# Where the split parts of the u/gate weights are kept, when their raw columns are loaded, and a Silu in two parts

## The chip, the cores and the metric

The kernel runs on one core of a Trainium2 chip. The metric is device time in microseconds (us) of one execution. In the text PE is the matrix engine (TensorE), DVE is VectorE, ACT is ScalarE, POOL is GpSimd, and SP is the engine whose queue issues the DMAs.

## The reference, cut to what matters

One inference step of a two-layer trunk over 1088 tokens (1024 of a prompt, 8 x 8 of new tokens), width 1024, fp32. Layer 0 is a gated linear attention and is the same before and after the change. Layer 1 is the one that matters here:

```
h = rmsnorm(x, norm_g[1])
u, v, gate = split(h @ w_in, 3)           # three times 1024 columns
v = layernorm(v, ln_g, ln_b)
mixed = ws (lower triangle, per group) @ v, within chunks of 128 positions, + bias
z = u * mixed * silu(gate)
x = x + z @ w_out
y = rmsnorm(x, norm_final)
```

## The kernel before

**Precision.** Each fp32 operand is split in two parts, `hi` (a copy that the matrix engine reads as fp32r) and `lo` (the rest). A split of a weight block of 128 x 1024 numbers is two halves of work: one ACT copy (`A.activation(w[:, 0], ...)`) and one DVE subtraction (`V.tensor_tensor(w[:, 1], ...)`). A product is three passes: hi.hi, hi.lo and lo.hi.

**The u/gate stage.** A loop over m = 0..7 makes u and gate for 128 columns each, and z for them. It doesn't do eight block products but seven, after Winograd's scheme: the weights of one m are cut in four quarters `q[1,1]`, `q[1,2]`, `q[2,1]`, `q[2,2]` (even and odd k-tiles by u and gate), POOL makes four sums of them (`sums`: s1 = q21+q22, s2 = s1-q11, s3 = q11-q21, s4 = q12-s2, 128 x 512 each), and the activations' sums `tsum` have been made before the loop. The seven products of one m run on the PE in this order, 24 matmuls of 272 columns each:

| product | weights | accumulator | what frees or reads the accumulator |
|---|---|---|---|
| 1 | s2 | `pb` | ACT copies it to `p6` (L1133, tile name `half`) |
| 2 | s3 | `pe` (tile `two`) | ACT copies it to `sg` (L1145) |
| 3 | s1 | `pb`, added to product 1 | DVE adds it to `sg` (L1149) |
| 4 | q11 | `pa` (tile `p1`) | ACT copies it to `p1` (L1156), POOL adds that to `p6` and `sg` (L1158, L1159) |
| mix | v by the spatial weights | two tiles `mix` in the tag "o" (two buffers), then a small third one for the sample tokens | DVE writes `zt` from each (L1102, L1096) |
| 5 | s4 | `pb` | DVE adds it to `p1` (L1174) |
| 6 | q22 | `pe` | DVE makes `sg` of the first half of the tokens from it (L1194) |
| 7 | q12 | `pa` | DVE multiplies it into `zt` (L1215) |

`sg` is the gate. It is multiplied by the tokens' 1/rms (`rs_all`), goes through Silu on ACT (L1198, all 1088 tokens at once), is multiplied by `rs_all` once more, and `zt` is multiplied by it (L1217) and spilled to DRAM (`z_spill`).

Seven tiles hold the split parts of one m (tag "w", eight buffers, `parts_of`, L964 and L965). They are taken **in turn**: each new split goes into the buffer that was used eight splits ago. The raw columns of the next m are loaded by `Quarters(...)` (L959, four DMAs of 256 KB) late in the iteration, after the Silu, into one tile `rawq`; POOL makes s1 and s2 of the next m after product 3, s3 and s4 later, and ACT and DVE split the parts of the next m between product 5 and the first products of the next m.

**What sets the order.** From the v stage to the end of the loop the order is that of the code: `in_order()` ties each instruction to the one before it on its own engine, so on every engine (the SP queue too) nothing passes an instruction that waits. After the loop a scheduler orders the instructions by priority.

**After the loop.** `out_proj(28, ...)` computes x + z @ w_out. Its blocks (p, m) are 24 matmuls for 128 output columns m and a piece p of the tokens (384, 384 or 320 of them), 24 blocks in all; `fm_block` takes an accumulator of the tag "mm" (two buffers, the tag that `pa` uses too). Blocks (0, 0) and (0, 1) come first. They need the four weight tiles of block 28, w28_0 to w28_3 (two k-tiles each, L122 and L123), and `zs[0]`, the splits of z for the first 384 tokens: k-tiles 0 to 4 come from `stage`, 5 and 6 from `rest` (both read back from the spill), 7 from the last `zt`. Even k-tiles can be split once product 3 of m = 7 is done, odd ones after product 5, since both overwrite `act_all`, which these products read. In the last iteration the order on DVE is therefore a mix of the gate's work, seven of these splits, and the splits of w28_0 to w28_2.

Of the kernel before, what the change touches and what calls it, by code (L numbers as in the profile page):

```python
# [40 lines left out]
def trunk_kernel(ctx: ExitStack, tc: tile.TileContext, a: dict):  # L41
# [67 lines left out]

    def load_w(blk, i):  # L110
        n = 256 + (LOW if blk == 1 else 0)
        raws[blk, i] = wp.tile([P, 2, 256 + LOW], F32, tag="raw", bufs=3, name=f"wr{blk}_{i}")[:, :, :n]
# [683 lines left out]
    def out_proj(base, act, resid, done, seq, gain=None):  # L796
# [29 lines left out]
        for item in seq:  # L826
# [141 lines left out]
    class Quarters:  # L968
# [19 lines left out]
        def parts(self, key):  # L988
            self.w[key] = parts_of(self.raw[key])

        def plain(self, *keys):
            for k in keys:
                self.w[k] = parts_of(self.q[k])
# [126 lines left out]
    for m in range(KT):  # L1120
# [9 lines left out]
        p6, p1 = ([tmp(t, 2, QUART, "half") for r in R] for t in ("sq", "hn"))  # L1130
        for r in R:
            product(pb[r], w["s2"], tq[1][r])
            A.activation(p6[r], pb[r], AF.Copy)  # L1133
# [45 lines left out]
        v_out(m, vm, bc)  # L1179
        if more:  # L1180
            nxt.sums("s4", up)
            vm = v_load(m + 1)
# [8 lines left out]
        for r in R:
            product(pe[r], w[2, 2], tq[3][r], start=False)
        for r in R:
            V.tensor_tensor(sg[:, qa[r]], p6[r], pe[r], ALU.add)  # L1194
        if more:
            nxt.plain((1, 1))
        V.tensor_tensor(sg[:, fa], sg[:, fa], rs_all[:, fa], ALU.mult)
        A.activation(sg, sg, AF.Silu)  # L1198
        if more:
            nxt.plain((2, 2))  # L1200
        else:
            fetch_w(28, [1, 2])
        V.tensor_tensor(sg[:, fa], sg[:, fa], rs_all[:, fa], ALU.mult)
        V.tensor_tensor(sg[:, fb], sg[:, fb], rs_all[:, fb], ALU.mult)
        if more:
            nxt.plain((1, 2))
            if m + 2 < KT:
                following = Quarters(22 + m)
            else:
                stage = mp.tile([P, 5, N], F32, tag="rawq", name="zstage")  # L1210
                SP.dma_start(stage, z_d[:, 0:5, 0:N])
                following = None
        for r in R:
            product(pa[r], w[1, 2], b21[r], start=False)
            V.tensor_tensor(zt[:, qa[r]], pa[r], zt[:, qa[r]], ALU.mult)  # L1215
# [157 lines left out]
```

## Time and profile before

| | us |
|---|---|
| median of 3 runs | 950.47 (947.46 to 951.05) |
| the profiled execution | 951.55, of which the span from first to last instruction is 949.8 |
| PE busy | 909.2 of the span |
| DVE, ACT, POOL busy | 630.6, 458.8, 279.8 |
| u/gate loop, first to last product | 636.7 to 829.7 |
| first matmul of `out_proj(28)` | 836.9 |
| start of the last matmuls of the kernel | 938.7 |

The profiled execution is 1.08 us longer than the median. Times in the text are those of its trace, counted from the start of the span. Rows of the timeline give start, duration, engine, line, operation, output and inputs, a count, and in brackets the idle time ahead of it with what ended it. For matmuls the duration of a row reaches to the end of the last one's pipeline, so distances between products are read from their starts.

### The profile page before, as it was taken

What the parts mean: (1) busy time and instruction counts of PE and PEld (TensorE: products, weight loads), DVE (VectorE), ACT (ScalarE), POOL (GpSimd) and SP (SyncE); (2) the same over time, 40 slices, a digit from 0 to 9 for tenths busy, and PEclk for the clock granted to TensorE, in tenths of its full rate; (3) what the DMA queues carried; (4) which work ended last, traced back from release to release, by engine and by line L of the source; (5) the groups of instructions that cost most, each with busy time, mean ns of one, the idle gap of its engine ahead of it and who ended that gap; (6) DMA issues with size and microseconds to landing.
All of it is one profiled execution on the core that took longest, in us unless ns stands there. A gap on an engine that the chain in (4) does not pass through costs nothing.

```text
span 949.8 us, 17088 instructions
## 1 busy us (share of the span) xinstructions
PE 909.2 (96%) x6437; PEld 882.1 (93%) x6437; DVE 630.6 (66%) x1288; ACT 458.8 (48%) x972; POOL 279.8 (29%) x307
## 2 busy tenths in 40 slices
PE   9989999999999999989999999999999999979995
PEld 8979989998999899978999999999999999879994
DVE  7888777577885877688544755465666666772246
ACT  7664644454462545464243545554444444463322
POOL 2023332323222342222242200025554554301123
PEclk9999999999999999999999999999999999979998
DMA  9302113310231212324583344552233233573233
GB/s 297 92 1 81 51 34 89 106 45 29 67 104 59 62 50 78 118 70 127 169 259 112 101 143 144 185 159 82 90 94 95 97 96 97 160 245 101 58 112 129
DMA packets 89968, 101.80 MB, mean 107 GB/s; under 512 B 9863, under 2 KB 80845, under 8 KB 89885
## 3 DMA queue, kind: packets, MB, share of 16 engines
q1 hardware_dynamic: 89884, 100.71, 34.1%
q8 instruction: 50, 0.82, 0.4%
q14 instruction: 34, 0.27, 0.1%
HBM read 74.26 MB, written 26.42 MB: 106 GB/s over the span
## 4 chain that ended last, share of the span: by engine, by line
PE 46%; DVE 24%; DMA 11%; issue 6%; ACT 6%; POOL 5%; SPq 2%; DVEq 0%; POOLq 0%; ACTq 0%
PE fm L137 26%; PE tm L151 10%; DVE wq L965 4%; DMA rawq<-w 3%; DMA xsum<-x_spill 3%; DMA wr<-w 1%; PE sc L513 1%; POOL qsum L977 1%; PE o L623 1%; PE pst L584 1%; SPq L959 1%; POOL half L1158 1%; DVE sg L1183 1%; DMA xt<-x_spill 1%; DVE scT L526 1%
## 5 line engine op out<-in xcount | busy, mean ns | idle before, releaser
L137 PE MATMUL fm<-act,w 128*128 128x384 f32 (+1 forms) x2208 | 390.7, 333 | 7.9 <-DVE zt L1215 7.0
L137 PEld LDWEIGHTS fm<-act,w 128*128 128x128 f32 x2208 | 368.1, 189 | 11.7 <-ACT act L197 7.2
L151 PE MATMUL tm<-w,act 128*128 128x256 f32 (+1 forms) x1536 | 193.1, 283 | 0.9 <-ACT vt L1010 0.6
L151 PEld LDWEIGHTS tm<-w,act 128*128 128x128 f32 x1536 | 185.5, 188 | 2.9 <-ACT vt L1010 1.1
L123 DVE TENSOR_TENSOR w<-wr,w 128x512 fp32r<-128x512 f32 (+1 forms) x96 | 68.1, 724 | 25.1 <-ACT w L122 24.5
L122 ACT ACTIVATE w<-wr 128x512 fp32r<-128x512 f32 (+1 forms) x96 | 58.5, 625 | 31.8 <-DMA wr<-w 19.7
L821 POOL TENSOR_TENSOR acc<-acc,sq 128x384 f32<-128x384 f32 (+1 forms) x30 | 30.4, 1014 | 117.6 <-ACT sq L816 117.2
L843 DVE TENSOR_TENSOR x<-fm,res 128x384 f32<-128x384 f32 (+1 forms) x40 | 21.0, 527 | 56.6 <-PE fm L137 56.6
L999 PE MATMUL pb<-act,wq 128*128 128x272 f32 x384 | 52.1, 292 | 5.3 <-ACT half L1133 5.2
L999 PEld LDWEIGHTS pb<-act,wq 128*128 128x128 f32 x384 | 48.9, 189 | 6.9 <-ACT half L1133 6.9
L816 ACT ACTIVATE sq<-x 128x384 f32<-128x384 f32 (+1 forms) x42 | 20.9, 503 | 63.8 <-DVE x L843 61.6
L999 PE MATMUL two<-tsum,wq 128*128 128x272 f32 x384 | 51.6, 290 | 0.0
L999 PE MATMUL p<-act,wq 128*128 128x272 f32 x384 | 51.0, 288 | 0.0
L999 PEld LDWEIGHTS p<-act,wq 128*128 128x128 f32 x384 | 49.4, 188 | 0.0
L999 PEld LDWEIGHTS two<-tsum,wq 128*128 128x128 f32 x384 | 49.1, 188 | 0.0
L977 POOL TENSOR_TENSOR qsum<-rawq 128x512 f32<-128x512 f32 x16 | 20.6, 1288 | 84.1 <-DMA rawq<-w 81.2
L468 POOL TENSOR_TENSOR xe<-xe,k 128x384 f32<-128x384 f32 (+2 forms) x24 | 29.1, 1212 | 44.3 <-ACT xe L467 41.1
L654 POOL TENSOR_TENSOR on<-on,g 128x384 f32<-128x384 f32 (+1 forms) x24 | 23.8, 1012 | 56.6 <-DVE on L653 34.6
L964 ACT ACTIVATE wq<-qsum 128x512 fp32r<-128x512 f32 x25 | 15.0, 626 | 52.3 <-POOL qsum L977 52.3
L444 POOL TENSOR_TENSOR kd<-kd,k 128x384 f32<-128x384 f32 (+1 forms) x12 | 12.0, 1002 | 85.8 <-ACT kd L443 85.8
L475 DVE TENSOR_TENSOR xl<-cum 128x192 f32<-128x192 f32 (+4 forms) x72 | 34.6, 507 | 0.0
L1102 DVE SCALAR_TENSOR_TENSOR zt<-mix,lng,bias 128x512 f32<-128x512 f32 x16 | 11.4, 747 | 31.9 <-DMA z_spill<-zt 21.3
(260 smaller groups left out, 1585.3 us busy)
## 6 DMA issues: line engine op xcount, KB each, us to landing
wr<-w SPq DMA_DIRECT2D x92, 256.0 KB, 3.1
rawq<-w SPq DMA_DIRECT2D x32, 256.0 KB, 3.8
xsum<-x_spill SPq DMA_DIRECT2D x16, 272.0 KB, 3.1
z_spill<-zt SPq DMA_DIRECT2D x8, 544.0 KB, 6.0
s<-s SPq DMA_DIRECT2D x16, 256.0 KB, 3.9
state_s<-ns SPq DMA_DIRECT2D x32, 128.0 KB, 2.5
v_spill<-vt SPq DMA_DIRECT2D x32, 128.0 KB, 2.7
vm<-v_spill SPq DMA_DIRECT2D x8, 512.0 KB, 4.2
```

What stands on the lines that cost most here:

```text
L122: A.activation(w[:, 0], raw, AF.Copy)
L123: V.tensor_tensor(w[:, 1], raw, w[:, 0].bitcast(F32), ALU.subtract)
L137: PE.matmul(acc, lhs, rhs, start=(k == 0), stop=(k == 23))
L151: PE.matmul(acc, lhs, rhs, start=(k == 0), stop=(k == 23))
L468: G.tensor_tensor(xe, xe, kt_[:, :nl], ALU.mult)
L475: V.tensor_tensor(l3[:, :, lo:hi], c3[:, :, (i + 1) * m:], r, ALU.subtract)
L654: G.tensor_tensor(o, o, gate[h][:, j, t0:t0 + n], ALU.mult)
L821: (V if gain is not None and p == 2 or m == KT - 1 else G).tensor_tensor(total, acc[p], sq, ALU.add)
L843: V.tensor_tensor(raw[p][:, m, :], pa, r, ALU.add)
L965: V.tensor_tensor(w[:, 1], src, w[:, 0].bitcast(F32), ALU.subtract)
L977: G.tensor_tensor(t, x, y, op)
L999: PE.matmul(acc, lhs, rhs, start=start and k + i == 0, stop=k + i == 5, skip_group_check=not start)
```

## The change

1. **Places.** A split of the next m goes into the tile of a product that has just been done, which is named in the code: q11 into the tile of s2 (after product 1), q22 into that of s3, q12 into that of s1, s2 into a spare eighth tile, s3 into that of q11, s1 into that of s4, s4 into that of q22; the tile of q12 is the next iteration's spare. The order of the splits changes with that: in iterations 1 to 6 they are spread over the whole iteration, and all four sums of the next m are made by POOL at its start.
2. **Load.** `Quarters(...)` for the m after the next is issued after product 4, no longer after the Silu; on the SP queue it stands ahead of the load of `vm` instead of behind it. `v_out` (two POOL operations and a DMA) moves from the end of the iteration to behind the normalisation of `vm`.
3. **Silu in two parts.** The second half of the tokens (`fb`) goes through `rs_all` and Silu before product 5, the first half (`fa`) after product 6.
4. **First iteration.** m = 0 has an order of its own: the raw columns for m = 1 arrive during it, its q11, q22 and q12 are split right after product 4, s3 and s4 are summed after the two POOL multiplications into `zt`.
5. **Hand-over to `out_proj(28)`.** The weights of blocks 28 to 31 are split into the eight tiles of the last m (`places`); w28_0 is loaded in m = 6 and split after product 3 of m = 7; the accumulators of blocks (0, 0) and (0, 1) come from the tag "o".

```diff
+    places = {}
...
     def fetch_w(blk, qs=range(4)):
...
+            if blk in places:
+                w = places[blk][i].rearrange("p s k c -> p s (k c)").rearrange("p s (k c) -> p s k c", k=2)
+            else:
+                w = wp.tile([P, 2, 2, 256 + LOW], F32R, tag="w", bufs=8, name=f"w{blk}_{i}")[:, :, :, :n]
...
-            pa = fm_block(ws_[base + m // 2], (m % 2) * P, act[p], p)
+            pa = fm_block(ws_[base + m // 2], (m % 2) * P, act[p], p, "o" if gain is not None and (p, m) < (0, 2) else "mm")
...
-        cur.parts("s4")
         if first:
-            for key in ((1, 2), (2, 2)):
-                cur.plain(key)
-            nxt = Quarters(21)
+            for key in ("s4", (2, 2), (1, 2)):
+                cur.parts(key)
+            nxt, spare = Quarters(21), place()
+        elif more:
+            for key in ("s1", "s2", "s3", "s4"):
+                nxt.sums(key, up if key == "s4" else None)
+        else:
+            places[28] = places[30] = [w["s2"], w["s3"], w["s1"], spare]
+            places[29] = places[31] = [w[1, 1], w["s4"], w[2, 2], w[1, 2]]
...
+        if mid:
+            nxt.parts((1, 1), w["s2"])
...
+        if mid:
+            nxt.parts((2, 2), w["s3"])
         v_norm(vm, range(0 if first else 4, 9))
+        v_out(m, vm, bc)
...
-        if more:
-            for key in ("s1", "s2"):
-                nxt.sums(key)
+        if mid:
+            nxt.parts((1, 2), w["s1"])
+            nxt.parts("s2", spare)
+        if not more:
+            fetch_w(28, [0])
...
+        if mid:
+            if m + 2 < KT:
+                following = Quarters(22 + m)
...
+        if first:
+            nxt.sums("s1")
+            nxt.sums("s2")
...
+        if first:
+            for key, at in (((1, 1), "s2"), ((2, 2), "s3"), ((1, 2), "s1")):
+                nxt.parts(key, w[at])
+        elif more:
+            nxt.parts("s3", w[1, 1])
+        else:
+            zs = [act_all[:, :, :, lo:lo + n] for lo, n in zip((T - N, 0, N), size)]
+            for kt in (0, 2, 4):
+                split(zs[0], kt, stage[:, kt, :])
         for c in range(2):
             mixed(zt, vm, g, m, bias, 4 * c)
+        V.tensor_tensor(sg[:, fb], sg[:, fb], rs_all[:, fb], ALU.mult)
+        A.activation(sg[:, fb], sg[:, fb], AF.Silu)
+        if first:
+            nxt.parts("s2", spare)
...
+        if first:
+            nxt.sums("s3")
+            nxt.sums("s4", up)
+            following = Quarters(22)
+        elif more:
+            nxt.parts("s1", w["s4"])
...
+        if first:
+            nxt.parts("s3", w[1, 1])
+            nxt.parts("s1", w["s4"])
         if more:
-            nxt.plain((1, 1))
+            nxt.parts("s4", w[2, 2])
         V.tensor_tensor(sg[:, fa], sg[:, fa], rs_all[:, fa], ALU.mult)
-        A.activation(sg, sg, AF.Silu)
+        A.activation(sg[:, fa], sg[:, fa], AF.Silu)
-        if more:
-            nxt.plain((2, 2))
-        else:
-            fetch_w(28, [1, 2])
+        if not more:
+            fetch_w(28, [1])
...
         if more:
             if m + 2 == KT:
-                rest = [wp.tile([P, N], F32, tag="raw", bufs=3, name="zmore") for _ in range(2)]
-                for i, t in enumerate(rest):
-                    SP.dma_start(t, z_d[:, 5 + i, 0:N])
-                load_w(28, 0)
+                SP.dma_start(rest[1], z_d[:, 6, 0:N])
+            spare = w[1, 2]
             cur, nxt = nxt, following
```

In the rows below `wq` is a tile of split parts, `qsum` and `qs` are sums by POOL, `rawq` the raw quarters.

ACT before, in a middle iteration, from the copies of product 4 (`half<-p`) to those of the next product 1 (`half<-pb`):

```order
L1156 ACTIVATE half<-p_8645 128x272
L1156 ACTIVATE half<-p_8646 128x272
L964 ACTIVATE wq<-qsum 128x512 x3
L964 ACTIVATE wq<-rawq 128x512
L1198 ACTIVATE sg<-sg 128x1088
L964 ACTIVATE wq<-rawq 128x512 x2
L1133 ACTIVATE half<-pb 128x272 x2
```

Two splits of `rawq` stand between the Silu and the copies of product 1. ACT after the change, in the same iteration, from the third raw split (q12):

```order
L972 ACTIVATE wq<-rawq 128x512
L972 ACTIVATE wq<-qsum 128x512
L1174 ACTIVATE half<-p_8637 128x272
L1174 ACTIVATE half<-p_8638 128x272
L972 ACTIVATE wq<-qsum 128x512
L1201 ACTIVATE sg<-sg 128x544
L972 ACTIVATE wq<-qsum 128x512
L972 ACTIVATE wq<-qs_8562 128x512
L1243 ACTIVATE sg<-sg 128x544
L1139 ACTIVATE half<-pb 128x272 x2
```

The raw splits have moved ahead of product 4's copies, and the copies of product 1 follow the second half of the Silu directly. DVE before, in iteration m = 0, from the addition of product 3:

```order
L1149 TENSOR_TENSOR sg<-sg,pb 128x272 x2
L1102 SCALAR_TENSOR_TENSOR zt<-mix,lng,bias 128x512 x2
L1174 TENSOR_TENSOR half<-half,pb 128x272 x2
L1096 SCALAR_TENSOR_TENSOR zt<-mix,lng,bias 128x64
L1183 TENSOR_TENSOR sg<-sg,rs 128x544
L965 TENSOR_TENSOR wq<-qsum,wq 128x512 x3
L1194 TENSOR_TENSOR sg<-half,two 128x272 x2
```

The reading of the two mix tiles follows product 3 at once. DVE after, in the same iteration:

```order
L1165 TENSOR_TENSOR sg<-sg,pb 128x272 x2
L973 TENSOR_TENSOR wq<-rawq,wq 128x512 x3
L1107 SCALAR_TENSOR_TENSOR zt<-mix,lng,bias 128x512 x2
L1200 TENSOR_TENSOR sg<-sg,rs 128x544
L973 TENSOR_TENSOR wq<-qsum,wq 128x512
L1210 TENSOR_TENSOR half<-half,pb 128x272 x2
L1101 SCALAR_TENSOR_TENSOR zt<-mix,lng,bias 128x64
L1215 TENSOR_TENSOR sg<-sg,rs 128x544
L1236 TENSOR_TENSOR sg<-half,two 128x272 x2
```

Three splits of the freshly loaded columns now stand ahead of the reading of the mix tiles. PE before, from the second half of the last product 7 into `out_proj(28)`; `fm_9701` is block (0, 0), `fm_9736` block (0, 1), and w28_0 to w28_3 are the weights:

```order
L999 MATMUL p1_9470<-act_80,wq_9327 128x272 x12
L137 MATMUL fm_9701<-act_80,w28_0_9523 128x384 x6
L137 MATMUL fm_9701<-act_80,w28_1_9599 128x384 x6
L137 MATMUL fm_9701<-act_80,w28_2_9602 128x384 x6
L137 MATMUL fm_9736<-act_80,w28_0_9523 128x384 x6
L137 MATMUL fm_9736<-act_80,w28_1_9599 128x384 x4
L137 MATMUL fm_9701<-act_80,w28_3_9640 128x384 x2
```

28 matmuls stand ahead of the first one with w28_3. PE after, at the same place; `fm_9657` is block (0, 0), `fm_9691` is (0, 1), `fm_9727` is (1, 0), and `wq_7366`, `wq_7468`, `wq_7471`, `wq_7292` hold w28_0 to w28_3:

```order
L1004 MATMUL p1_9434<-act_80,wq_7479 128x272 x12
L142 MATMUL fm_9657<-act_80,wq_7366 128x384 x6
L142 MATMUL fm_9657<-act_80,wq_7468 128x384 x2
L142 MATMUL fm_9691<-act_80,wq_7366 128x384 x2
L142 MATMUL fm_9657<-act_80,wq_7468 128x384 x4
L142 MATMUL fm_9657<-act_80,wq_7471 128x384 x2
L142 MATMUL fm_9691<-act_80,wq_7366 128x384 x4
L142 MATMUL fm_9691<-act_80,wq_7468 128x384 x2
L142 MATMUL fm_9657<-act_80,wq_7471 128x384 x4
L142 MATMUL fm_9691<-act_80,wq_7468 128x384 x4
L142 MATMUL fm_9691<-act_80,wq_7471 128x384 x6
L142 MATMUL fm_9727<-act_80,wq_7366 128x384 x6
```

Behind these come four more matmuls of (1, 0), and then the first one with w28_3: 46 matmuls stand ahead of it, of three blocks.

More of the change, by code (lines that the diff above doesn't have):

```diff
@@ L960, in raw_quarters, with place, parts_of @@
         return rw
-    def parts_of(src):
-        w = wp.tile([P, 2, 4, P], F32R, tag="w", bufs=8, name="wq")
+    def place():
+        return wp.tile([P, 2, 4, P], F32R, tag="w", bufs=8, name="wq")
+    def parts_of(src, w=None):
+        w = w if w is not None else place()
         A.activation(w[:, 0], src, AF.Copy)
@@ L986, in sums, with parts @@
             r[key] = self.sum(x, y, op, into)
[L988 to L993, printed above, removed]
+        def parts(self, key, into=None):
+            self.w[key] = parts_of(self.raw[key] if key in self.raw else self.q[key], into)
     def product(acc, w, b, start=True):
@@ L1130, in trunk_kernel @@
         p6, p1 = ([tmp(t, 2, QUART, "half") for r in R] for t in ("sq", "hn"))
+        mid = more and not first
         for r in R:
@@ L1156, in trunk_kernel @@
             A.activation(p1[r], pa[r], AF.Copy)
+        if mid:
+            if m + 2 < KT:
+                following = Quarters(22 + m)
+            else:
+                stage = mp.tile([P, 5, N], F32, tag="rawq", name="zstage")
+                SP.dma_start(stage, z_d[:, 0:5, 0:N])
+                following = None
+        if first:
+            nxt.sums("s1")
+            nxt.sums("s2")
         for r in R:
@@ L1178, in trunk_kernel @@
         G.tensor_tensor(zt[:, qb[1]], zt[:, qb[1]], p1[1], ALU.mult)
[L1179 to L1182, printed above, removed]
         V.tensor_tensor(sg[:, fb], sg[:, fb], rs_all[:, fb], ALU.mult)
         if more:
-            for key in ("s2", "s3", "s1"):
-                nxt.parts(key)
-        else:
-            for kt in (1, 3, 5):
-                split(zs[0], kt, stage[:, kt, :] if kt < 5 else rest[kt - 5])
+            vm = v_load(m + 1)
+        if first:
[4 more added lines that the diff above has]
+            nxt.parts("s1", w["s4"])
+            if m + 2 == KT:
+                load_w(28, 0)
+                rest = [wp.tile([P, N], F32, tag="raw", bufs=3, name="zmore") for _ in range(2)]
+                SP.dma_start(rest[0], z_d[:, 5, 0:N])
+        else:
+            split(zs[0], 5, rest[0])
             load_w(28, 3)
+            for kt in (1, 3):
+                split(zs[0], kt, stage[:, kt, :])
         for r in R:
@@ L1194, in trunk_kernel @@
             V.tensor_tensor(sg[:, qa[r]], p6[r], pe[r], ALU.add)
+        if first:
+            nxt.parts("s3", w[1, 1])
+            nxt.parts("s1", w["s4"])
         if more:
[L1196 removed]
+            nxt.parts("s4", w[2, 2])
         V.tensor_tensor(sg[:, fa], sg[:, fa], rs_all[:, fa], ALU.mult)
[L1198 to L1212 removed]
+        A.activation(sg[:, fa], sg[:, fa], AF.Silu)
+        if not more:
+            fetch_w(28, [1])
+        V.tensor_tensor(sg[:, fa], sg[:, fa], rs_all[:, fa], ALU.mult)
         for r in R:
@@ L1215, in trunk_kernel @@
             V.tensor_tensor(zt[:, qa[r]], pa[r], zt[:, qa[r]], ALU.mult)
+        if not more:
+            fetch_w(28, [2])
         for part in ((slice(0, T),) if more else (slice(0, N), slice(N, T))):
```

9 lines of the change are left out of this document (3 added, 6 removed).

## The prediction

> **What bounds the kernel now.** I read the page's head first, then what the PE waited for, longest in total first (us in total, times, longest).
>
> ```profile
> span 949.8 us, 17088 instructions
> PE 909.2 (96%) x6437; PEld 882.1 (93%) x6437; DVE 630.6 (66%) x1288; ACT 458.8 (48%) x972; POOL 279.8 (29%) x307
> ...
> PE fm L137 <- DVE zt L1215: 7.0, 1, 7.0
> PE pb L999 <- ACT half L1133: 5.2, 6, 1.2
> ```
>
> The PE is the bound; only its waits can be won. The two longest lie in what the change touches: one before `out_proj(28)`, six ahead of product 3. Next, the eight iterations as stretches (start:end, length, busy PE, PEld, DVE, ACT, POOL, clock), then the PE in m = 4:
>
> ```profile
> 636.70:660.20 23.50, 23.50 (x189) 23.26 (x187) 13.20 (x30) 13.48 (x30) 9.31 (x11) 1.00 0.29 84
> ...
> sum 193.04, PE 187.55 PEld 185.48 DVE 125.62 ACT 87.26 POOL 91.64; mean PE 23.44 PEld 23.19 DVE 15.70 ACT 10.91 POOL 11.46
> ...
> 736.14 3.21 PE L999 MATMUL two<-tsum,wq 128*128 128x272 f32 x24
> 740.53 3.27 PE L999 MATMUL pb<-act,wq 128*128 128x272 f32 x24 [1.19 <-ACT half L1133]
> ...
> 757.72 3.17 PE L999 MATMUL pb<-tsum,wq 128*128 128x272 f32 x24
> 760.74 3.17 PE L999 MATMUL two<-tsum,wq 128*128 128x272 f32 x24
> ```
>
> A product without a wait takes 3.02 (757.72 to 760.74). Product 3 to the next product 2 takes 20.21 (740.53 to 760.74), so an iteration can't be shorter than 20.21 + 3.02 = 23.23. Eight of them are 185.84 against 193.04: 7.2 too long. 0.27 of it is m = 0's start, which stays. **6.9 can be won in the loop.** Who is late there, DVE and ACT in m = 4:
>
> ```profile
> 733.14 2.12 DVE L965 TENSOR_TENSOR wq<-qsum,wq 128x512 fp32r<-128x512 f32 x2
> 735.18 0.77 DVE L1194 TENSOR_TENSOR sg<-half,two 128x272 f32<-128x272 f32 x2
> 735.88 1.50 DVE L965 TENSOR_TENSOR wq<-rawq,wq 128x512 fp32r<-128x512 f32 x1
> 737.30 0.71 DVE L1197 TENSOR_TENSOR sg<-sg,rs 128x544 f32<-128x544 f32 x1
> ...
> 738.05 1.12 ACT L1198 ACTIVATE sg<-sg 128x1088 f32<-128x1088 f32 x1 [4.89 <-DVE sg L1197]
> 739.07 1.13 ACT L964 ACTIVATE wq<-rawq 128x512 fp32r<-128x512 f32 x2
> 740.10 0.66 ACT L1133 ACTIVATE half<-pb 128x272 f32<-128x272 f32 x2
> ```
>
> Splits queue on DVE ahead of the gate, so Silu is late; two splits on ACT follow it, and only then is product 1's accumulator copied, which product 3 adds to (due 739.16, started 740.53).
>
> The hand-over to `out_proj(28)`, PE, DVE and SP, and the granted clock (the value behind POOL's):
>
> ```profile
> 826.72 3.18 PE L999 MATMUL p<-act,wq 128*128 128x272 f32 x24
> 836.93 71.90 PE L137 MATMUL fm<-act,w 128*128 128x384 f32 x408 [7.03 <-DVE zt L1215]
> 908.67 0.81 PE L809 MATMUL ssq<-total,ones_r 128*128 128x384 f32 x2
> ...
> 831.39 0.72 DVE L1197 TENSOR_TENSOR sg<-sg,rs 128x544 f32<-128x544 f32 x1
> 833.87 1.29 DVE L123 TENSOR_TENSOR w<-wr,w 128x512 fp32r<-128x512 f32 x2 [1.75 <-ACT w L122]
> 842.27 0.69 DVE L123 TENSOR_TENSOR w<-wr,w 128x512 fp32r<-128x512 f32 x1
> 852.55 0.56 DVE L843 TENSOR_TENSOR x<-fm,res 128x384 f32<-128x384 f32 x1
> 856.76 0.56 DVE L843 TENSOR_TENSOR x<-fm,res 128x384 f32<-128x384 f32 x1 [1.85 <-PE fm L137]
> 860.31 0.49 DVE L843 TENSOR_TENSOR x<-fm,res 128x320 f32<-128x320 f32 x1 [2.99 <-PE fm L137]
> ...
> 831.00:832.00 1.00, 0.00 (x0) 0.00 (x0) 0.97 (x3) 0.00 (x0) 0.00 (x0) 1.00 0.12 33
> 833.00:834.00 1.00, 0.00 (x0) 0.00 (x0) 0.13 (x1) 1.00 (x3) 0.00 (x0) 0.50 0.88 319
> 842.00:843.00 1.00, 1.00 (x5) 1.00 (x4) 1.00 (x3) 1.00 (x3) 0.00 (x0) 0.54 0.97 405
> 843.00:844.00 1.00, 1.00 (x8) 1.00 (x7) 1.00 (x3) 0.14 (x1) 0.00 (x0) 1.00 0.18 70
> ```
>
> The last product ends at 826.72 + 3.02 = 829.74: 7.2 idle. The clock fell to 0.50 about 3 us later and stayed there until 842.9. A block of 384 columns takes 4.21 (852.55 to 856.76), one of 320 takes 3.55. The 408 matmuls are 13 and 4 blocks: 68.9, against 908.67 - 836.93 = 71.7, so 2.8 went to the half clock. **10.0 can be won here.** Behind it the PE works on almost without a wait, so what is won moves the end.
>
> **The change, part by part.**
>
> *Loop, m = 2 to 6: 0 waits left.* Count from product 1's start: product 6 ends at 20.2, DVE makes the gate's half by 21.0 (0.77). s4's split on ACT is at most 0.63 and on DVE at most 1.50, ending 22.5; the multiplication by `rs` 0.71, doubled if a POOL sum runs beside it, 24.0; a half Silu at most the whole one's 1.12, 25.1. The copies of product 1 then wait only for product 1 (second half done 26.3) and end at 26.9; product 3 is due at 29.3. Slack 2.4. A split into a tile just used makes ACT wait for the PE (q12 for product 3, s1 for product 5, s4 for product 6); behind it queue product 4's copies and the Silu halves, with over 1 us to spare each by the same count. The second Silu instruction costs ACT a few tenths; ACT idles 4.89 there.
>
> *The load: 0.*
>
> ```profile
> 742.35 1.76 SPq L959 DMA_DIRECT2D rawq<-w  x4
> 748.13 1.28 POOL L977 TENSOR_TENSOR qsum<-rawq 128x512 f32<-128x512 f32 x1 [11.04 <-DMA rawq<-w]
> ```
>
> 5.8 from request to first sum. On SP it now waits behind `v_out` and for q12's split, to about 12 in the iteration, so it lands at 18, and the sums start at 20; they are wanted from 26 on. `vm` behind it on SP waited anyway for the sample mix at 17.
>
> *m = 0: a new wait, 2.3.* DVE now does three raw splits ahead of reading the mix tiles, and the third mix tile reuses the first one's buffer.
>
> ```profile
> 651.01 1.28 POOL L977 TENSOR_TENSOR qsum<-rawq 128x512 f32<-128x512 f32 x1 [10.22 <-DMA rawq<-w]
> ...
> 650.23 1.65 DVE L1102 SCALAR_TENSOR_TENSOR zt<-mix,lng,bias 128x512 f32<-128x512 f32 x2 [3.40 <-PE mix L1101]
> 653.93 0.33 PE L1095 MATMUL mix<-wss,vm 128*128 128x64 f32 x2
> 658.32 3.31 DVE L965 TENSOR_TENSOR wq<-qsum,wq 128x512 fp32r<-128x512 f32 x3
> 661.91 1.28 POOL L977 TENSOR_TENSOR qs<-rawq,qsum 128x512 f32<-128x512 f32 x1
> 662.25 1.49 DVE L965 TENSOR_TENSOR wq<-rawq,wq 128x512 fp32r<-128x512 f32 x1
> ```
>
> The columns land at 651.0, ACT has the first copy at 651.6. At 1.49 for the split beside a sum and 1.10 (3.31/3) for the other two, DVE is through at 655.3, the first mix tile is read by 656.2 (1.65/2), and the sample mix, at 653.93 before, waits 2.3. Without any interference (the three bound by ACT's 0.56 each, then one plain DVE split) it is about 0.5; I take 2.3, since POOL sums at just that time. The rows 661.91 and 662.25 show the interference: the split ends 0.55 after the sum. [...]
>
> *m = 1: 2.0.* s4's sum stands behind both POOL multiplications now and ends about 665.6 (663.2 before). Three splits, `rs` and Silu behind it put product 1's copies 1.0 late. The load for m = 2 waits for that sum and lands at 671.4 (+5.8); `vm`'s normalisation, the splits and the mix reading run late by it, and the sample mix loses another 1.0. Bounds 0 and 3.0. Last iteration: three z splits ahead of the mix reading, 0.3 (0 to 0.5).
>
> Loop: 6.9 - 2.3 - 2.0 - 0.3 = **2.3 won** (0.3 to 6.4).
>
> *Hand-over: 6.7 won.* With the accumulators in "o" and w28_0 split early, the PE starts block (0, 0) as product 7 ends. It has 6 matmuls (1.05), then needs w28_1, which ACT splits after the last Silu. Before, the gate's multiplication (L1197) ended 2.4 after the last product; DVE is now relieved of w28_0 there (0.69) but multiplies the other half earlier (0.71). I take 1.5 to 2.4, plus half a Silu and a split (1.2): w28_1 at 2.8, a wait of 1.7 (1.0 to 2.9). From there DVE needs some 8 us of rows of 0.55 to 0.9 until w28_3 (before: 835.2 to 843.0), about 11 after the last product; the PE's 46 matmuls ahead of it end at 9.8: 1.3 more, and 0.3 between. Together 3.3 (2.3 to 5.5) of the 10.0 stay. No wait here nears the 3 us after which the clock fell, so the 2.8 go too. [...]
>
> Sum: 2.3 + 6.7 = 9.0 off the profiled 951.55, 942.5; that execution is 1.08 above the median, so **941.5** on the scale of the runs.
>
> **Rivals.**
> [...]
> 2. *The change doesn't do what it says in the loop*: product 1's copies stay late, because the four sums now run beside the gate's end. The loop keeps its 6.9 and gets the new 4.6, the hand-over gives 6.7: 948.4. Against: 2.4 of slack.
> 3. *Slower.* The same place, full strength: s4's split, two `rs` multiplications and the final `zt` of every iteration each wait 1.28 for a sum, 5.1 in all, 2.7 beyond the slack, in six iterations 16. With 4.6 in the other three and 6.9 gone, 6.7 from the hand-over: 957.5. It decides when Silu's second half ends later than 28.5 in an iteration; I get 25.1.
> 4. *More than forecast*: m = 0 waits 0.5, m = 1 nothing, hand-over 2.3: 6.4 + 7.7 won, 936.4.
>
> **How the numbers follow.** Half a per cent (4.75 us) is about what a measurement here can tell from no change. Chances: forecast 0.65, rival 4 0.12 (both faster, 0.77), rival 1 0.11 and rival 2 0.06 (same, 0.17), rival 3 0.06 (slower). The range, 936.5 to 947.5, runs from the lower bound of the unknown costs over rival 1; it leaves out most of rivals 2 and 3 and the edge of 4.
>
> **What would show it.** Iterations 2 to 6 at 23.2 to 23.3 with no wait on L1139; a PE wait at the sample mix (L1100) on DVE's L1107 in m = 0, of about 2.3, and smaller ones in m = 1; the first L142 matmul within 0.3 of product 7's end; waits of 1 to 3 at w28_1 and w28_3 (ACT L127, DVE L128) and a clock of 1.00 throughout. Wrong it would be with a wait ahead of product 3 in every iteration, or a 0.50 clock after the hand-over.

## The result and the profile after

The changed kernel takes 942.74 us (median of 7 runs, 941.70 to 945.41), the one before 950.47 (7 runs, 947.46 to 955.96). The ratio is 0.992, 95% interval 0.9892 to 0.9949: faster by 0.8%. The forecast was 941.5 with a range of 936.5 to 947.5. The profiled execution took 944.72, 2.0 above the median; the profiled one of before 951.55.

The page's head after, and the PE's waits from the loop's start to 850 (us in total, times, longest):

```profile
span 942.9 us, 17092 instructions
...
PE 905.1 (96%) x6437; PEld 880.3 (93%) x6437; DVE 640.8 (68%) x1288; ACT 462.6 (49%) x980; POOL 285.4 (30%) x307
...
PE mix L1100 <- DVE zt L1107: 5.5, 2, 3.3
PE fm L142 <- ACT wq L127: 1.3, 1, 1.3
```

Both waits of before are gone (7.0 ahead of the last projection, 5.2 ahead of product 3). Two take their place: at the sample mix (the third, small mix tile, of the sample tokens), twice, and at w28_1. The iterations as stretches (start:end, length, busy PE, PEld, DVE, ACT, POOL, clock):

```profile
637.71:663.65 25.94, 23.75 (x189) 23.32 (x187) 16.84 (x35) 14.63 (x31) 9.76 (x11) 1.00 0.32 99
663.65:693.36 29.71, 26.28 (x189) 25.88 (x187) 23.54 (x29) 12.15 (x27) 20.54 (x21) 0.89 0.34 112
693.36:716.47 23.11, 23.11 (x188) 23.11 (x187) 15.48 (x25) 10.92 (x24) 12.02 (x13) 1.00 0.31 100
...
sum 194.33, PE 188.71 PEld 187.88 DVE 135.87 ACT 91.27 POOL 96.92; mean PE 23.59 PEld 23.48 DVE 16.98 ACT 11.41 POOL 12.11
```

m = 2 to 7 take 23.11 or 23.12 each, with the PE never idle: all that they could win. m = 0 and m = 1 give back more than that, so the eight take 194.33 against 193.04. The hand-over on the PE:

```profile
829.02 3.19 PE L1004 MATMUL p<-act,wq 128*128 128x272 f32 x24
832.04 1.22 PE L142 MATMUL fm<-act,wq 128*128 128x384 f32 x6
834.54 13.71 PE L142 MATMUL fm<-act,wq 128*128 128x384 f32 x77 [1.28 <-ACT wq L127]
...
901.91 0.81 PE L814 MATMUL ssq<-total,ones_r 128*128 128x384 f32 x2
```

The first block starts as product 7 ends. From product 7's start to the first ssq matmul are 72.89 us; before they were 908.67 - 826.72 = 81.95. So the span's 6.9 are: +1.0 ahead of the loop (first product at 637.71, before at 636.68), +1.3 in the loop, -9.06 at the hand-over, -0.1 behind it.

m = 0 and m = 1, on DVE, PE, SP and POOL:

```profile
652.41 4.08 DVE L973 TENSOR_TENSOR wq<-rawq,wq 128x512 fp32r<-128x512 f32 x3 [4.57 <-ACT wq L972]
656.42 1.40 DVE L1107 SCALAR_TENSOR_TENSOR zt<-mix,lng,bias 128x512 f32<-128x512 f32 x2
657.30 0.41 PE L1100 MATMUL mix<-wss,vm 128*128 128x64 f32 x2 [2.19 <-DVE zt L1107]
...
665.27 1.30 POOL L985 TENSOR_TENSOR qs<-rawq,qsum 128x512 f32<-128x512 f32 x1
666.60 1.75 SPq L964 DMA_DIRECT2D rawq<-w  x4
671.61 1.97 POOL L985 TENSOR_TENSOR qsum<-rawq 128x512 f32<-128x512 f32 x1 [5.04 <-DMA rawq<-w]
678.90 4.68 DVE L973 TENSOR_TENSOR wq<-qsum,wq 128x512 fp32r<-128x512 f32 x2
683.51 1.40 DVE L1107 SCALAR_TENSOR_TENSOR zt<-mix,lng,bias 128x512 f32<-128x512 f32 x2
684.39 0.66 PE L1100 MATMUL mix<-wss,vm 128*128 128x64 f32 x2 [3.33 <-DVE zt L1107]
684.82 5.68 PE L1004 MATMUL two<-tsum,wq 128*128 128x272 f32 x24
```

In m = 0 three raw splits stand on DVE ahead of the mix reading, as forecast. In m = 1 the load for m = 2 is requested only when s4's sum has ended (666.57), 2.95 behind the start of m = 1; four sums and three raw splits (splits of raw columns, not of sums) follow its landing, and two splits that take 2.34 each stand ahead of the mix reading. Product 6 behind that wait takes 5.5 instead of 3.1: the granted clock was 0.50 from 683.41 to 690.24.

### The profile page after: what moved, and what is told of

Same layout as the page of the kernel before. It is cut to its first block, busy times and chain, and to the rows that moved or that the text cites. A ratio compares the mean times of both kernels' runs of the same rounds, so it can differ in the third digit from the quotient of the medians.

```text
span 942.9 us, 17092 instructions
## 1 busy us (share of the span) xinstructions
PE 905.1 (96%) x6437; PEld 880.3 (93%) x6437; DVE 640.8 (68%) x1288; ACT 462.6 (49%) x980; POOL 285.4 (30%) x307
## 4 chain that ended last, share of the span: by engine, by line
PE 67%; DVE 14%; DMA 5%; issue 5%; ACT 5%; POOL 3%; SPq 1%; DVEq 0%; ACTq 0%; POOLq 0%
PE fm L142 28%; PE tm L156 12%; PE pb L1004 6%; PE two L1004 5%; PE p L1004 4%; DMA xsum<-x_spill 3%; PE sc L518 2%; PE pst L589 1%; PE o L628 1%; PE o L597 1%; DVE act L203 1%; DVE scT L531 1%; PE mix L1106 1%; PE first L285 1%; PE o L599 1%
## 5 line engine op out<-in xcount | busy, mean ns | idle before, releaser
L142 PE MATMUL fm<-act,w 128*128 128x384 f32 (+1 forms) x1632 | 290.2, 332 | 0.4 <-DVE act L203 0.4
L142 PEld LDWEIGHTS fm<-act,w 128*128 128x128 f32 x1632 | 269.8, 188 | 2.4 <-DVE act L203 0.6
L142 PE MATMUL fm<-act,wq 128*128 128x384 f32 (+1 forms) x576 | 96.6, 328 | 1.7 <-ACT wq L127 1.3
L142 PEld LDWEIGHTS fm<-act,wq 128*128 128x128 f32 x576 | 94.7, 188 | 3.2 <-ACT wq L127 1.6
L128 DVE TENSOR_TENSOR w<-wr,w 128x512 fp32r<-128x512 f32 (+1 forms) x80 | 57.3, 732 | 16.7 <-ACT w L127 16.1
L127 ACT ACTIVATE w<-wr 128x512 fp32r<-128x512 f32 (+1 forms) x80 | 48.7, 624 | 24.9 <-DMA wr<-w 13.2
L1004 PE MATMUL two<-tsum,wq 128*128 128x272 f32 x384 | 54.2, 299 | 0.1
L1004 PEld LDWEIGHTS two<-tsum,wq 128*128 128x128 f32 x384 | 51.7, 197 | 0.3 <-DVE wq L973 0.3
L973 DVE TENSOR_TENSOR wq<-qsum,wq 128x512 fp32r<-128x512 f32 x25 | 27.6, 1112 | 12.4 <-ACT wq L972 12.2
```

The costliest lines, as they stand in the source:

```text
L127: A.activation(w[:, 0], raw, AF.Copy)
L128: V.tensor_tensor(w[:, 1], raw, w[:, 0].bitcast(F32), ALU.subtract)
L142: PE.matmul(acc, lhs, rhs, start=(k == 0), stop=(k == 23))
L973: V.tensor_tensor(w[:, 1], src, w[:, 0].bitcast(F32), ALU.subtract)
L1004: PE.matmul(acc, lhs, rhs, start=start and k + i == 0, stop=k + i == 5, skip_group_check=not start)
```

## The experiments

The instructions ahead of the loop are the same in all these kernels, yet its first product starts anywhere from 635.6 to 642.1; so the kernels are compared by stages. "Request" is the start of the load for m = 2 against the start of m = 1; "m = 1 wait" is that at its sample mix; "end" is the loop's start to the span's end; "hand-over" is product 7's start to the first ssq matmul. Times in us from one profiled execution, the ratio (to the kernel before) from timed runs.

| kernel | m = 0 | m = 1 | request | m = 1 wait | hand-over | end | ratio, 95% |
|---|---|---|---|---|---|---|---|
| before | 23.52 | 23.88 | | 0 | 81.95 | 313.1 | 1 |
| changed | 25.94 | 29.71 | +2.95 | 3.33 | 72.89 | 305.2 | 0.992 (0.9892 to 0.9949) |
| mix_first | 24.22 | 31.80 | +4.81 | 3.37 | 73.13 | 305.8 | 0.9914 (0.9881 to 0.9946) |
| sums_sooner | 25.94 | 23.12 | -2.07 | 0 | 72.97 | 298.7 | 0.9856 (0.9823 to 0.9889) |
| both_early | 25.02 | 25.53 | -1.24 | 1.54 | 72.89 | 300.1 | 0.9859 (0.9825 to 0.9893) |
| adds_first | 25.34 | 23.70 | -1.82 | 0 | 72.32 | 298.1 | 0.9868 (0.9844 to 0.9891) |
| raws_late | 23.52 | 27.43 | +0.27 | 1.82 | 72.89 | 300.5 | 0.9902 (0.9882 to 0.9923) |
| last_silu | 25.10 | 23.12 | -2.05 | 0 | 71.99 | 296.9 | 0.9882 (0.9860 to 0.9905) |
| one_silu | 25.25 | 27.72 | +1.12 | 2.63 | 72.35 | 302.0 | 0.9914 (0.9888 to 0.9941) |
| late_load | 29.19 | 24.32 | +0.15 | 1.02 | 73.01 | 303.2 | 0.9935 (0.9915 to 0.9956) |
| acc_mm | 27.15 | 27.07 | +1.40 | 2.22 | 77.11 | 308.0 | 0.9979 (0.9958 to 1.0001) |
| before_o | 23.52 | 23.67 | | 0 | 77.93 | 306.4 | 0.9954 (0.9931 to 0.9977) |

In every kernel with the changed loop, late_load among them, m = 2 to 6 take 23.08 to 23.12. Not so m = 0 and m = 1: the changed kernel and acc_mm have the same code there and take 55.65 and 54.22 for both together, sums_sooner and last_silu, the same as each other too, 49.06 and 48.22. So a difference of some 1.5 in this sum tells nothing by itself; the 5.2 and more between these two pairs does.

### m = 0 and m = 1

**mix_first.** In m = 0 the mix reading ahead of the raw splits:

```diff
         if first:
-            for key, at in (((1, 1), "s2"), ((2, 2), "s3"), ((1, 2), "s1")):
-                nxt.parts(key, w[at])
+            pass
...
         for c in range(2):
             mixed(zt, vm, g, m, bias, 4 * c)
+        if first:
+            for key, at in (((1, 1), "s2"), ((2, 2), "s3"), ((1, 2), "s1")):
+                nxt.parts(key, w[at])
```

> In m = 0 DVE reads the two mix tiles ahead of the three raw splits, all else as in the changed kernel. Theory 1 (the order of the first iterations costs what the trace shows): the PE's wait at the sample mix in m = 0, 2.2 us in the changed kernel, goes to 0.3 or less, and m = 0 takes about 23.7 instead of 25.9. The three splits end about 1.4 later, and nothing that the PE waits for is near them; the sums s3 and s4 on POOL come at the same time, so the wait of 3.3 in m = 1 and the half clock behind it stay. Span about 940.7, 2.2 below the changed kernel's 942.9. Rival: the splits that now come later hold the gate's half Silu and the copies of product 1, the wait moves to product 3 of m = 1, and the span stays at 942.5 to 943.

The PE's waits in 650 to 700:

```profile
PE mix L1100 <- DVE zt L1107: 3.4, 1, 3.4
PE two L1004 <- ACT wq L972: 1.0, 1, 1.0
PE two L1004 <- DVE wq L973: 0.6, 1, 0.6
PE pb L1004 <- DVE half L1212: 0.5, 1, 0.5
```

m = 0's wait at the sample mix went, so the splits were its cause; the wait in m = 1 stayed. But 2.1 came back at products 1 and 2 of m = 1: at product 5's additions on DVE and at s3's split, whose sum stands behind POOL's multiplications. m = 0 and m = 1 together take 56.0, before the edit 55.65. The rival was right on the total, though it had the wrong place; the span's 1.5 less is the loop's earlier start (635.58).

**sums_sooner.** In m = 0 s3 and s4 summed ahead of POOL's multiplications into `zt`:

```diff
         if first:
+            nxt.sums("s3")
+            nxt.sums("s4", up)
+        if first:
...
-            nxt.sums("s3")
-            nxt.sums("s4", up)
             following = Quarters(22)
```

> In m = 0 POOL makes the sums s3 and s4 of the next m ahead of the two multiplications into zt, not behind them, so that the raw tile is free and the load for m = 2 is requested sooner. Theory 1 (m = 1 is late because that load is): the load is requested about 5 us sooner (661.7 instead of 666.6) and lands at about 666.5; the wait of 3.3 at the sample mix of m = 1 falls below 1, no half clock follows, and m = 1 takes 23.1 to 24 instead of 29.7. The wait of 2.2 in m = 0 stays, or grows by up to 1, since two more sums run beside the splits. Span about 937 (936.5 to 938.5). Rival (m = 1 is late for the number of splits and sums that meet there, not for the time of the load): the wait of m = 1 stays above 2.5 and the span within 1.5 of 942.9.

m = 0 and m = 1:

```profile
638.71:664.65 25.94, 23.75 (x188) 23.32 (x187) 16.68 (x33) 16.10 (x34) 11.67 (x13) 1.00 0.36 106
664.65:687.77 23.12, 23.12 (x189) 23.12 (x187) 22.02 (x31) 10.45 (x24) 18.69 (x18) 1.00 0.40 135
```

As theory 1 had it: the wait and the half clock of m = 1 are gone, 6.6 us, with DVE still busy for 22.0 of 23.1. The request came at 662.58 against a forecast of 661.7. The interval lies wholly below that of the changed kernel: this version beats both.

**both_early**, the two edits together.

> The two edits together: in m = 0 s3 and s4 are summed ahead of POOL's multiplications into zt, and DVE reads the mix tiles ahead of the three raw splits. Theory 1: the eight iterations take 185.5 to 187.5 instead of 194.3 (m = 0 at 23.5, m = 1 at 23.1 to 24, the others at 23.1), the span is about 935 (934 to 936.5), and the time about 0.8% below the changed kernel's. Rival (the waits move instead of going): the loop stays above 190 and the span above 938.5.

m = 0 and 1 take 50.55 together, no less than the 49.06 with the sums alone (the medians of the timed runs are the same, 939.01): the wait of m = 0 moved to product 1 of m = 1 (1.35, on product 5's additions), and 1.54 came back in m = 1. The rival's mechanism (waits move) is shown; by size (loop 189.2, span 938.6) the result lies between the two.

**adds_first** and **raws_late** try to win the remaining 2.4 of m = 0 by other orders of the same work. Both put POOL's four additions ahead of all four sums. adds_first, against sums_sooner (the two mix readings part in every iteration, the rest is m = 0 alone):

```diff
-        if first:
-            nxt.sums("s1")
-            nxt.sums("s2")
         for r in R:
             G.tensor_tensor(p6[r], p6[r], p1[r], ALU.add)
             G.tensor_tensor(sg[:, qb[r]], sg[:, qb[r]], p1[r], ALU.add)
         if first:
-            nxt.sums("s3")
-            nxt.sums("s4", up)
+            for key in ("s1", "s2", "s3", "s4"):
+                nxt.sums(key, up if key == "s4" else None)
+        mixed(zt, vm, g, m, bias, 0)
         if first:
             for key, at in (((1, 1), "s2"), ((2, 2), "s3"), ((1, 2), "s1")):
                 nxt.parts(key, w[at])
...
-        for c in range(2):
-            mixed(zt, vm, g, m, bias, 4 * c)
+        mixed(zt, vm, g, m, bias, 4)
...
-        if first:
-            nxt.parts("s2", spare)
...
                 G.tensor_tensor(zt[:, qb[r]], zt[:, qb[r]], p1[r], ALU.mult)
+        if first:
+            nxt.parts("s2", spare)
```

> As the run with the sums sooner, and besides: DVE reads the first mix tile ahead of the splits that stand there and the second behind them; in m = 0 POOL adds product 4 to p6 and sg ahead of all four sums, and s2 is split behind product 5's additions instead of ahead of them. Theory 1, as the run of both edits changed it (two chains end at about the same time in m = 0: splits, then mix reading, then the sample mix; and s1 and s2, POOL's additions, rs, Silu, s2's split, then product 5's addition, for which product 1 of m = 1 waits): with both chains cut, m = 0 takes 23.5 to 23.8 and m = 1 23.1 to 23.6, the eight iterations 185.4 to 186.2 against 187.75 with the sums alone, and the span from the loop's start falls by 1.6 to 2.3. Rival (the splits and sums of m = 0 take DVE and POOL longer together than there is time, in whatever order): the loop stays at 187 or more, with the wait at product 1 or 2 of m = 1.

raws_late has the same order on POOL and leaves both mix readings together; its other edit, against sums_sooner:

```diff
-        if first:
-            for key, at in (((1, 1), "s2"), ((2, 2), "s3"), ((1, 2), "s1")):
-                nxt.parts(key, w[at])
...
-        if first:
-            nxt.parts("s2", spare)
...
                 G.tensor_tensor(zt[:, qb[r]], zt[:, qb[r]], p1[r], ALU.mult)
+        if first:
+            for key, at in (((1, 1), "s2"), ((2, 2), "s3"), ((1, 2), "s1")):
+                nxt.parts(key, w[at])
+            nxt.parts("s2", spare)
```

> As the run with the sums sooner, and besides in m = 0: POOL adds product 4 to p6 and sg ahead of all four sums, and the three raw splits stand behind product 5's additions on ACT and DVE, ahead of s2's split, no longer ahead of the mix reading. Theory (m = 0 has one wait because the raw splits, slowed by POOL, stand ahead of something that the PE wants; 5 us later nothing wanted stands behind them, if they end ahead of 23.5 from the loop's start): no wait at the sample mix, m = 0 takes 23.5 to 24.2; the raw tile is free at about 22.5 to 23, so the load for m = 2 is requested 0.5 to 1.5 ahead of the start of m = 1 (2.07 with the sums alone, where m = 1 waited nothing; 0.15 behind it in the run with the late load, where m = 1 waited 1.0), and m = 1 waits 0 to 1.5: 23.1 to 24.6. Both together 47.0 to 48.3 against 49.06. Rival (as the run with the additions first: the work of m = 0 on DVE and POOL, each slowed by the other, is what is too long): both together 48.8 to 50.5, with the wait at product 1 or 2 of m = 1.

DVE and POOL in adds_first; then m = 0 and m = 1 in raws_late; then DVE and SP there:

```profile
657.19 6.66 DVE L973 TENSOR_TENSOR wq<-rawq,wq 128x512 fp32r<-128x512 f32 x3 [0.97 <-ACT wq L972]
659.97 1.63 POOL L985 TENSOR_TENSOR qsum<-qsum,rawq 128x512 f32<-128x512 f32 x1
661.57 1.73 POOL L985 TENSOR_TENSOR qsum<-rawq 128x512 f32<-128x512 f32 x1
```

```profile
640.60:664.12 23.52, 23.52 (x189) 23.28 (x187) 15.71 (x29) 16.12 (x34) 11.05 (x12) 1.00 0.36 106
664.12:691.55 27.43, 25.16 (x189) 24.75 (x188) 25.81 (x34) 10.36 (x24) 18.46 (x18) 0.94 0.37 122
```

```profile
659.72 4.60 DVE L973 TENSOR_TENSOR wq<-rawq,wq 128x512 fp32r<-128x512 f32 x3 [0.56 <-ACT wq L972]
664.39 1.75 SPq L964 DMA_DIRECT2D rawq<-w  x4
```

In adds_first the three splits take 2.2 each beside the sums (0.68 alone) and s2's split comes 1.5 late for product 1: 49.04 for m = 0 and m = 1, as with the sums alone. In raws_late m = 0 has no wait at all, but the raw tile is free only at 664.3, and m = 1 pays: 50.95. Here the sums had ended at 662.6; it is the raw tile, freed late by the splits, that held the request. So what m = 1 needs is the load in time, as far as these runs go (none moves the request without a sum or a split): with a request 2 ahead of its start it waited nothing (sums_sooner, last_silu, adds_first), from -1.2 to +1.4 between 1.0 and 2.6, from +3 on 3.3. Both rivals were right: the work of m = 0 on DVE and POOL, each slowed by the other, can be shifted (in adds_first a split took 2.2 for 0.68, a sum 1.73 for the mean 1.29 of before), but no order tried here brought m = 0 and m = 1 clearly under the 49.06 and 48.22 with the sums alone; the kernel before took 47.40 there.

### The load

**late_load.** The load issued behind the last Silu again, in m = 1 to 5:

```diff
-            if m + 2 < KT:
-                following = Quarters(22 + m)
-            else:
+            if m + 2 == KT:
...
         V.tensor_tensor(sg[:, fa], sg[:, fa], rs_all[:, fa], ALU.mult)
+        if mid and m + 2 < KT:
+            following = Quarters(22 + m)
```

> The changed kernel with the load of the raw columns for the m after the next issued behind the last Silu in m = 1 to 5, as the kernel before has it, no longer behind product 4. Theory 1 (the new order of the splits, all four sums at the start of an iteration, needs the sooner load): the sums start 6 to 8 later, and the mix, product 1 and the half Silus behind the splits that wait for them are late; each of m = 2 to 6 takes 2 to 4 longer than 23.11, with waits at L1100 or L1139, and the span is 10 to 20 longer, 953 to 963. Rival (the sooner load is not needed, since the columns wait for their turn anyway): m = 2 to 6 stay at 23.1 to 23.2 and the span within 1 of 942.9.

SP and POOL around the start of m = 2, then m = 2 as a stretch:

```profile
688.30 1.88 SPq L964 DMA_DIRECT2D rawq<-w  x4
695.24 2.17 POOL L985 TENSOR_TENSOR qsum<-rawq 128x512 f32<-128x512 f32 x1 [4.75 <-DMA rawq<-w]
```

```profile
693.00:716.12 23.12, 23.12 (x189) 23.12 (x188) 15.38 (x25) 11.32 (x25) 14.04 (x13) 1.00 0.32 106
```

Theory 1 fell. The load for m = 3 is requested 4.7 ahead of m = 2's start, its first sum starts 2.2 into it, and the iteration has no wait. In m >= 2 the sooner load is worth nothing. (m = 0, the same code as in the changed kernel, took 29.19 here because its wait of 2.63 was followed by half clock.)

### Silu and the hand-over

**one_silu.** One Silu over all tokens behind product 6, and the second multiplication of the other half by `rs` behind it:

```diff
-        A.activation(sg[:, fb], sg[:, fb], AF.Silu)
...
-        V.tensor_tensor(sg[:, fb], sg[:, fb], rs_all[:, fb], ALU.mult)
...
-        A.activation(sg[:, fa], sg[:, fa], AF.Silu)
+        A.activation(sg, sg, AF.Silu)
...
+        V.tensor_tensor(sg[:, fb], sg[:, fb], rs_all[:, fb], ALU.mult)
```

> The changed kernel with one Silu over all 1088 tokens behind product 6, and both multiplications by rs around it, no longer in two parts. Theory 1 (the loop has slack at product 3, forecast at 2.4): m = 2 to 6 stay at 23.1, since the whole Silu is 0.5 longer than the half and the multiplication of the other half adds 0.7 behind it; the hand-over has the whole Silu and its second multiplication ahead of w28_1 and loses 0.4 to 1.2. Span 0.4 to 1.5 longer, m = 0 and m = 1 within 1 of the changed kernel's. Rival (the two parts are what made the copies of product 1 punctual): a wait on L1139 ahead of product 3 in every iteration, as in the kernel before, of 0.3 to 1.2, and 3 to 6 in the loop.

No wait ahead of product 3 in any iteration: the split in two isn't what made product 1's copies punctual. With late_load, which rules out the load, that leaves the places and the new order of the splits and sums; no run takes these apart. At the hand-over the sign was wrong: 72.35, 0.5 less than with two parts.

**last_silu**, the sums sooner and a whole Silu in m = 7 alone.

> As the run with the sums sooner, with the Silu of m = 7 alone in one part again. Theory (the half Silu of m = 7 stands on ACT ahead of three splits of z, DVE waits 1.1 for these, and the gate's end, w28_1 behind it, is late by that; in the run with one Silu the gate ended 2.4 behind product 7's start and w28_1 held nobody, in the changed kernel 4.3 and it held the PE 1.3): no wait at w28_1, and from product 7's start to the first ssq matmul 72.3 to 72.5 instead of 72.97; iterations 0 to 6 as with the sums sooner. Rival (in the run with one Silu it was the loop's other course, not the last Silu): 72.9 to 73.1 with the wait of 1.3. By time the two differ by 0.05%, which only the trace tells.

DVE of the changed kernel ahead of the gate's end, then last_silu's PE and DVE:

```profile
827.50 0.56 DVE L203 TENSOR_TENSOR act<-zmore,act 128x384 fp32r<-128x384 f32 x1 [1.14 <-ACT act L202]
832.55 0.73 DVE L1242 TENSOR_TENSOR sg<-sg,rs 128x544 f32<-128x544 f32 x1
```

```profile
824.59 3.19 PE L1004 MATMUL p<-act,wq 128*128 128x272 f32 x24
827.62 8.72 PE L142 MATMUL fm<-act,wq 128*128 128x384 f32 x45
826.26 0.73 DVE L1244 TENSOR_TENSOR sg<-sg,rs 128x544 f32<-128x544 f32 x1
```

As the theory had it. With the half Silu ahead of the z splits on ACT, DVE stood 1.14 idle and the gate's multiplication ended 4.26 behind product 7's start; with the whole one it ends 2.40 behind, and no wait is left. The 71.99 are what 408 matmuls and product 7 take (68.9 + 3.0). No timed difference from sums_sooner can be told (939.08 and 939.01).

**acc_mm.** The accumulators of blocks (0, 0) and (0, 1) from the old tag; **before_o** is the opposite: the kernel before with only these accumulators from "o".

```diff
-            pa = fm_block(ws_[base + m // 2], (m % 2) * P, act[p], p, "o" if gain is not None and (p, m) < (0, 2) else "mm")
+            pa = fm_block(ws_[base + m // 2], (m % 2) * P, act[p], p, "mm")
```

This is acc_mm; before_o has the two lines the other way round, in the kernel before.

> The changed kernel with the accumulators of blocks (0, 0) and (0, 1) from the tag that the last product uses, as before the change; places, load, Silu and early weights stay. Theory 1: the first matmul of the block waits for the multiplication that reads the last product's second accumulator or the first one's (the two halves of product 7), which end after the last product, so the first matmul starts 1 to 4 us behind product 7's end; after a wait of more than 3 the clock is at 0.50 for some 6 us again (2.5 to 3 lost). What of the wait at w28_1 (1.3) lay behind it falls into it. Span 3 to 6 longer, 946 to 949. Rival: the early weights alone make the hand-over, because the multiplication of the first half is done by then, and the span stays within 0.5 of 942.9.

> The kernel before with one edit: blocks (0, 0) and (0, 1) of the last projection take their accumulators from the tag "o". Theory 1 (the accumulators alone don't make the hand-over): w28_0 is split on DVE behind the gate there, from 833.9, about 4 behind the last product, so the first matmul starts 4.5 to 5 behind product 7's end instead of 7.2, the clock is at 0.50 when it does (some 2 to 2.8 lost), and the 6 matmuls of w28_0 end before w28_1 is split. The hand-over wins 1.5 to 4 of the 9.1 that the whole change won. Rival 1 (the accumulator was all of it): 8 to 9 won. Rival 2 (the early weights are all of it): 0 to 0.5. The loop stays at 193.

The PE in acc_mm, then in before_o:

```profile
831.97 3.18 PE L1004 MATMUL p<-act,wq 128*128 128x272 f32 x24
839.30 9.02 PE L142 MATMUL fm<-act,wq 128*128 128x384 f32 x42 [4.15 <-DVE zt L1249]
```

```profile
829.83 1.20 PE L137 MATMUL fm<-act,w 128*128 128x384 f32 x6
833.86 12.43 PE L137 MATMUL fm<-act,w 128*128 128x384 f32 x53 [2.84 <-ACT w L122]
```

The accumulators are worth 4.2 with the rest of the change (77.11 to 72.89) and 4.0 without it (81.95 to 77.93), some 45% of the 9.06. The clock of acc_mm was at half for 3.41 us behind its wait, which cost some 0.8 (its 408 matmuls took 69.78, against 68.9), less than expected; its span is longer than forecast since its loop started at 642.12. By time acc_mm can't be told from the kernel before (0.9958 to 1.0001), though it is 5.1 shorter from the loop's start on: in the profiled execution its loop started 5.4 later. In before_o the first block starts at once too: w28_0 was already split when product 7 ended, against what I expected, and the 4.0 came by another course than the 1.5 to 4 of the forecast. The trace of the kernel before shows it as well; the two splits at 833.87, which I took for those of w28_0, are those of w28_1 and w28_2:

```profile
825.68 0.69 DVE L123 TENSOR_TENSOR w<-wr,w 128x512 fp32r<-128x512 f32 x1 [1.25 <-ACT w L122]
```

So the accumulators alone let the first block start; whether w28_0's earlier split helps otherwise, by relieving DVE ahead of the gate, no run shows. The other 5.0 are mostly the wait for w28_1 (2.84 there, 1.28 in the changed kernel) and the half clock that followed it there (6.83 us, some 3 lost). before_o also shows how far one profile carries: its iterations 0 to 6, the same code as before, take 2.2 less (166.20, before 168.38). The 1.3 that the changed kernel's loop lost is less than that.

## Why the prediction was right, and where it was wrong

The time was right, 942.7 for 941.5, partly by luck: two errors cancelled. On the profiled execution the forecast was 942.5 and 944.72 came: 3.6 worse in the loop, 2.4 better at the hand-over, 1.0 worse ahead of the loop, where nothing was changed.

- *Loop, m = 2 to 6: 0 waits left.* Right. The floor is 23.11, not 23.23. Slack wasn't measured; one_silu took up some of it unseen.
- *The load: 0.* Right for m = 2 to 6 (late_load), and as forecast its time matters in one place, m = 1.
- *m = 0: 2.3.* Right: 2.19, gone with the splits moved. That it cost no more is luck: with the same code there acc_mm and late_load waited 1.87 and 2.63, the clock fell, and m = 0 took 3.6 and 5.7 more than the 23.52 of raws_late. The trace lies by the interference row: the three splits took 4.08 together (1.49 and twice 1.10 are 3.69). The loop's lower bound of 0.3 has 3.1 for this wait, a term that no run shows: the longest wait at this place was late_load's 2.63. In adds_first, however, 2.2 for each split beside POOL sums (0.68 alone) comes near a split and a whole sum one after the other (an estimate: 0.68 and a sum of 1.63 or 1.73 are 2.3 to 2.4).
- *m = 1: 2.0, bounds 0 and 3.0.* This term failed: m = 1 takes 6.6 over the floor (4.0 in acc_mm, with the same code there). The landing was right (forecast 671.4, first sum 671.61), and product 3 lost 0.4 instead of 1.0. What failed is the next step, "the sample mix loses another 1.0": it waited 3.3, since from 671.6 to 683.0 POOL worked almost without a break beside the splits ahead of it, first on the four sums, then on `v_out` and product 4's additions (20.5 us of POOL in m = 1, against 12.0 in m = 2). In sums_sooner DVE and POOL were nearly as busy (22.0 and 18.7) and nothing waited, with the first sum 3.2 into m = 1 instead of 8.0: it is the late start that makes this overlap cost. Another 2.4 are the half clock behind that wait, for which the sum had no term.
- *m = 7: 0.3.* It was 0.
- *Hand-over: 6.7.* 9.06. Mechanism right, but for w28_0, which needed no earlier split to be in time; the remainder was mis-sized: w28_1 held the PE 1.28 (forecast 1.7), w28_3 not at all (1.3), nothing between (0.3).
- *"No wait here nears the 3 us after which the clock fell."* Wrong as a rule, see below. It held at the hand-over, where the clock stayed at 1.00 and the first L142 matmul came within 0.1 of product 7's end (832.04), and failed in m = 1.

Of the rivals, none came. With the measured loop and only the forecast's 6.7 at the hand-over the time would have been 945.1.

## What to carry to other kernels

When the steady state of a loop is put in order, look at the first iterations by themselves: here all that six iterations won went to the first two, and summing two tiles sooner, so that the next load went out 5 us sooner, won 0.6%. Moving the work that a single wait names only handed the wait to the next product; moving the request that everything behind it needs removed it. And a PE wait should be priced with the clock: some 2 us cost little more than themselves in one run (2.19, and m = 0 was 2.42 longer than the 23.52 without a wait) and nearly twice that in another (1.87 in acc_mm, and 3.63), where the clock fell to 0.50 behind them.

## What the runs showed of the hardware

The clock. The changed kernel in stretches of 3.41 us (length, PE busy, ... , clock), two around the wait in m = 0, then four around that in m = 1:

```profile
652.69:656.10 3.41, 2.42 (x20) 2.20 (x18) 3.41 (x3) 2.02 (x3) 3.33 (x4) 1.00 0.00 0
656.10:659.52 3.42, 2.22 (x18) 2.25 (x19) 2.44 (x4) 0.16 (x1) 2.47 (x3) 1.00 0.13 34
676.59:680.00 3.41, 3.41 (x31) 3.41 (x30) 2.84 (x4) 2.28 (x6) 3.33 (x4) 1.00 0.01 2
680.00:683.41 3.41, 1.07 (x9) 0.85 (x7) 3.41 (x1) 0.00 (x0) 3.04 (x5) 1.00 0.42 112
683.41:686.83 3.42, 2.44 (x11) 2.47 (x12) 3.42 (x8) 1.18 (x2) 0.87 (x2) 0.50 0.67 242
686.83:690.24 3.41, 3.41 (x17) 3.41 (x17) 1.66 (x2) 0.00 (x0) 3.19 (x4) 0.50 0.43 126
```

The ten half-clock spells measured in these traces from the loop's start to 850 last 3.41, 6.83 or 10.24 us, one, two or three times 3.41; the one of before, from 832.70, is 10.24, of which the first 4 were idle. In acc_mm three of them start at 661.65, 688.95 and 839.14, 8 and 44 times 3.413 apart: in that trace they lie on one grid. In these ten the stretch ahead of every fall was busy for 0 to 48% (here 1.07 of 3.41); a stretch that was then busy for 95% or more (3.24 of 3.41 in acc_mm) ended the spell, one with up to 85% (2.91 in mix_first) did not. The wait in m = 0, 2.19, fell across two stretches, which stayed busy for 71 and 65%, and cost no clock; the wait of 1.87 in acc_mm's m = 0 did (45% busy). In the changed kernel's m = 1 such a stretch cost the working PE 1.4 to 1.5 us (an estimate: 17 matmuls in 686.83 to 690.24, against 29 in the stretch behind it and 31 in 676.59 to 680.00).

Ahead of the loop, the same instructions ended up to 6.5 us apart (635.6 to 642.1): as much as the whole change. What makes that difference stays open. Without stages a single profile would not have told these kernels apart.
